# The order estimate of a mixed attention and recurrence kernel: the lo halves of the weights booked on VectorE instead of GpSimd

## The chip, the cores and the metric

The kernel runs on one core of a Trainium2 chip. The metric is the device time of one execution in microseconds (us), the median of several timed runs. A difference of 0.3% (about 2.6 us) is what a measurement of this kernel can tell from no change. The profile is one further execution, taken by the hardware profiler.

## The reference

One layer over 528 tokens (16 learned tokens ahead of 512) of width 1024. A projection with 5384 columns of the normalised input feeds three parts: an RWKV-7 recurrence (8 heads), a forgetting attention (8 heads) and two sigmoid gates. The two branches are projected, gated and added, go through another projection into the residual, and a squared-ReLU MLP of width 4096 follows.

```python
h = jnp.concatenate([meta_b, x], axis=1)
u = rmsnorm(h, norm_mix[l])
proj = u @ w_in[l]
gates = jax.nn.sigmoid((proj[..., C_RW + C_FX:] + b_gate[l]).astype(jnp.float32))
y_rw = rwkv7_branch(feat_rw, ...)      # S_t = S_{t-1} (diag(w_t) + a_t^T b_t) + v_t^T k_t
y_fx = fox_branch(feat_fx, ...)        # softmax(q k^T + F_q - F_k), causal
merged = gates[..., :D_MODEL] * (y_rw @ w_out_rw[l]) + gates[..., D_MODEL:] * (y_fx @ w_out_fx[l])
h = h + (merged @ w_o[l]).astype(h.dtype)
z = rmsnorm(h, norm_mlp[l])
h = h + (jnp.square(jax.nn.relu(z @ w_up[l])) @ w_down[l]).astype(h.dtype)
return h[:, N_META:]
```

## The kernel before

Every large product is made of three passes: an operand is split into a rounded part `hi` and a rest `lo`, and `hi*hi`, `hi*lo` and `lo*hi` are added in PSUM. For a weight tile of 128x512 ScalarE makes `whi` (a cast, L470) and VectorE `wlo` (raw minus `whi`, L471). A block of the input projection (128 output columns) takes 8 slices of the contraction, three matmuls each, over the tokens in one part (128x512) or two (128x264); these are the rows `pj` of L501.

Work in order of time: the norm and the first two blocks of the projection; then the **mixed stage** (from `turns.add` at L1017 to `turns.run()` at L1024), in which the other 40 blocks, the recurrence and the attention share the engines; then the gated output projections (`po` of L1060, L1092, L1109), and the MLP (L1139, L1257).

In the mixed stage TensorE's instructions stand in exactly the order in which the program issues them (`manual_schedule`, L1023). That order is chosen while the kernel is built, by `Turns.run` (L164). Each stream of work is a generator that yields a function telling when its next step could start. Ranks give precedence: 0 is the chain over the chunks, 1 the rest of the recurrence, 2 the attention, 3 its features, 4 the group norm, 8 the projections, which so fill what is left. `run` takes the first stream, by rank, whose estimated start (plus a small allowance per rank, `ROOM`) isn't later than TensorE's estimated time `ck.pe`; if there is none, it takes the earliest and moves `ck.pe` to it, so that the estimate has TensorE wait there.

The estimated times are kept by `Clock`. Its `read` (L98) goes over each new instruction, takes the time at which its inputs are ready, and books it on its engine: `RATE` (L67) has a fixed cost and a cost per column for VectorE (0.18 us + 1.06 ns), ScalarE (0.25 us + 0.85 ns) and GpSimd (0.30 us + 2.1 ns). `book` (L88) takes the first gap on the engine that is long enough; steps of rank 0 and 1 are `urgent` and may be booked ahead of something that is booked already. For a projection's step the estimate asks for the time of `whi` and `wlo` (`ck.ready(*w[k // 4])`, L495). The other engines' order, their semaphores and the DMA queues follow from the order of the program and a priority for the urgent steps.

The parts that the prediction speaks of:

- `pairs`: heads go in pairs through `keys` (`pkk` L735), `rows`, `scores` (`psr` L788, taken out of PSUM by VectorE at L789 and L791) and `keys_turned` (`pbt` L802). Two pairs make a group; there are two groups.
- `inverse` (L806), once for each group: it inverts triangular blocks. VectorE transposes (L821, after the last `pbt`, since its tile lies where `BK` lay), goes through 15 steps of two dependent instructions (L832, L833), transposes twice (L835, L836) and spreads the result into `Tt` and `Dn` (four instructions of L841). Only then TensorE's first `pw` (L847) can start.
- `attention`: scores `psc` L607, a softmax on VectorE and ScalarE (L616 to L623), transposes `ppt`/`ppm` (L636, L638), the product `py` (L649, L652).
- After the stage `yhi` and `ylo` (L1045) are made of the results, the gates `gl` are loaded (L1054) and go through a tanh (L1055), and the weights `wraw` of `wout` are loaded and split (L232 to L236). The tiles of this part lie in memory that the mixed stage used, so their first writers wait for its last readers: `ylo` for the last `pj` matmul that reads `uhi`, `gl` for the tiles of the attention.

Of the kernel before, what the change touches and what calls it, by code (L numbers as in the profile page):

```python
# [61 lines left out]
class Clock:  # L62
# [35 lines left out]
    def read(self):  # L98

        new = self.nc.cur_bb.bb.instructions[self.seen:]  # L100
        self.seen += len(new)
        for x in new:
            outs = [o.bass_ap for o in x.outs if hasattr(o, "bass_ap")]
            ins = [o.bass_ap for o in x.ins if hasattr(o, "bass_ap")]
            if not outs:
                continue
            for o in outs:
                t = o.tensor
                if hasattr(t, "cap_key") and t.name not in self.free:
                    ring, n = self.rings.setdefault(str(t.cap_key).rsplit("_", 2)[0], []), t.tag_meta.bufs  # L110
                    self.free[t.name] = self.last(ring[-n]) if len(ring) >= n else 0.0
                    ring.append(t.name)
            names = [a.tensor.name for a in ins]
            out = outs[0].tensor.name
            eng = "Pool" if out.startswith("wlo") else str(x.engine).split(".")[-1]

            def cols(a):
                return math.prod(n for _, n in a.ap[1:])
            deps = max([self.w.get(n, 0.0) for n in names] + [self.free.get(out, 0.0)])
            if eng == "PE":  # L120
                n = max(cols(outs[0]), 64)
                big = tuple(x.tile_size) == (128, 128)
                if ins[0].dtype == F32R:
                    cost = n / 2400 + 0.013
                else:
                    cost = n / 600 if big else n / 1200
                if self.form != tuple(x.tile_size):
                    self.form = tuple(x.tile_size)
                    cost += 0.1
                self.pe = end = max(self.pe, deps) + cost  # L130
            else:
                size = max([cols(a) for a in outs + (ins if "Reduce" in str(x.opcode) else [])])
                if eng in self.RATE and "DMA" not in str(x.opcode):
                    fixed, per = self.RATE[eng]
                    end = self.book(eng, max(deps, self.last(out)), fixed + per * size) + fixed + per * size
                else:
                    cost = 0.3 + size * 128 * 4 / 2.0e5
                    end = self.book("DMA", max(deps, self.last(out)), cost) + cost + 2.0
            for o in outs:
                self.w[o.tensor.name] = max(self.w.get(o.tensor.name, 0.0), end + self.HOP)  # L140
            for n in names:
                self.r[n] = max(self.r.get(n, 0.0), end + self.HOP)
# [1245 lines left out]
```

## Time and profile before

| | |
|---|---|
| time, median of 3 runs | 881.36 us (881.16 to 883.7) |
| the profiled execution: its time, its span | 884.7 us, 882.9 us |
| mean granted TensorE clock | 0.988 |
| busy in the span | TensorE 852.5, VectorE 619.7, ScalarE 459.1, GpSimd 122.1 us |
| mixed stage | about 36 to 448 us |
| output projections, MLP | about 450 to 548 us, 548 us to the end |

The profile's page gives busy time by engine, then 40 slices of the span, DMA queues, the chain of work that ended last, and groups of instructions with the idle time ahead of them and what ended it. The views of the trace used here: the list of who waited for whom; the timeline, whose rows have start and length in us, engine, line, operation, `out<-in`, shape, and in brackets the idle time before and what ended it; the chain of waits, whose pieces have start, length, engine and line; and busy time by stretch. Matmuls overlap, so a piece of several matmuls divided by their number is what one costs, not the duration that a single row shows. A `pj` matmul with fp32 operands split as above is one instruction; the small fp32 matmuls count twice or more in the trace (x24 in the trace for 12 in the program).

### The profile page before, as it was taken

The numbers are of one execution on the slowest core, as the hardware profiler recorded it, in microseconds if no ns is written. First come the engines' busy times: TensorE is split into PE (matmuls) and PEld (weight loads), VectorE is DVE, ScalarE is ACT, GpSimd is POOL, SyncE is SP. The second block draws the span as 40 slices with busy tenths as digits, with TensorE's granted clock in tenths as the row PEclk, the third lists the DMA queues.
The fourth block names the chain that finished last, engine by engine and source line by source line (L and its number), as shares of the span: only waits on it lengthen the run. The fifth ranks groups of instructions, "written<-read, shape, count | busy, mean of one in ns | idle before, by whom it ended". The sixth has DMA issues, their size and how long they took to land.

```text
span 882.9 us, 15881 instructions
## 1 busy us (share of the span) xinstructions
PE 852.5 (97%) x6040; PEld 695.1 (79%) x6040; DVE 619.7 (70%) x1222; ACT 459.1 (52%) x943; POOL 122.1 (14%) x129
## 2 busy tenths in 40 slices
PE   7899999999999999999979899999999999999998
PEld 6887887778887876778768688988888888887886
DVE  6985786657877846655566655677777778767787
ACT  7756443865564427654365553465445434534452
POOL 1111100101101000000002200200720270055000
PEclk9989999999999999999999999999999999999999
DMA  6131123121121322213077550562663274326331
GB/s 217 50 96 48 49 72 104 25 76 50 40 60 50 113 74 73 74 37 108 25 262 231 164 189 1 160 199 60 210 188 103 60 238 156 96 87 223 108 97 71
DMA packets 51340, 95.91 MB, mean 109 GB/s; under 512 B 5816, under 2 KB 6968, under 8 KB 51264
## 3 DMA queue, kind: packets, MB, share of 16 engines
q1 hardware_dynamic: 47680, 86.52, 31.1%
q0 software_dynamic: 1280, 4.20, 1.5%
q10 hardware_dynamic: 2304, 4.20, 1.3%
q8 instruction: 47, 0.77, 0.4%
q14 instruction: 29, 0.24, 0.1%
HBM read 88.57 MB, written 6.31 MB: 107 GB/s over the span
## 4 chain that ended last, share of the span: by engine, by line
PE 82%; DVE 6%; DMA 3%; ACT 2%; issue 1%; POOL 0%; SPq 0%; DVEq 0%; ACTq 0%; POOLq 0%
PE pj L501 27%; PE po L1139 20%; PE po L1257 11%; PE pd L1257 5%; PE po L1109 2%; PE po L1092 2%; PE pw L847 2%; PE psc L607 1%; DMA gl<-gd 1%; PE pbt L802 1%; PE py L652 1%; DMA wraw<-in_wup 1%; DVE L L791 1%; DMA wraw<-in_wout 1%; PE pssq L553 1%
## 5 line engine op out<-in xcount | busy, mean ns | idle before, releaser
L501 PE MATMUL pj<-uhi,whi 128*128 128x264 f32 (+1 forms) x480 | 167.9, 350 | 0.0
L501 PE MATMUL pj<-ulo,whi 128*128 128x264 f32 (+1 forms) x480 | 156.5, 326 | 2.6 <-DVE ulo L401 2.6
L501 PE MATMUL pj<-uhi,wlo 128*128 128x264 f32 (+1 forms) x480 | 156.1, 325 | 0.0
L501 PEld LDWEIGHTS pj<-uhi,whi 128*128 128x128 f32 x480 | 92.3, 192 | 19.8 <-issue 11.1
L501 PEld LDWEIGHTS pj<-ulo,whi 128*128 128x128 f32 x480 | 92.8, 193 | 7.1 <-DVE ulo L401 3.0
L501 PEld LDWEIGHTS pj<-uhi,wlo 128*128 128x128 f32 x480 | 92.5, 193 | 7.1
L236 DVE TENSOR_TENSOR wlo<-wraw,whi 128x512 fp32r<-128x512 f32 x88 | 71.3, 821 | 35.0 <-ACT whi L235 34.5
L1139 PE MATMUL po<-zhi,whi 128*128 128x512 f32 (+1 forms) x248 | 94.9, 383 | 0.6 <-ACT whi L235 0.6
L1139 PE MATMUL po<-zhi,wlo 128*128 128x512 f32 (+1 forms) x248 | 94.9, 383 | 0.0
L1139 PE MATMUL po<-zlo,whi 128*128 128x512 f32 (+1 forms) x248 | 94.8, 382 | 0.0
L471 DVE TENSOR_TENSOR wlo<-wraw,whi 128x512 fp32r<-128x512 f32 x80 | 56.6, 713 | 38.2 <-ACT whi L470 37.2
L235 ACT CAST whi<-wraw 128x512 fp32r<-128x512 f32 x88 | 53.9, 618 | 53.9 <-PE po L1139 21.3
L470 ACT CAST whi<-wraw 128x512 fp32r<-128x512 f32 x80 | 49.1, 619 | 37.1 <-PE pj L501 29.9
L270 ACT CAST whi<-t 128x512 fp32r<-128x512 f32 x64 | 40.0, 624 | 44.5 <-DVE wlo L271 20.6
L1257 PE MATMUL po<-wlo,fhi 128*128 128x512 f32 x160 | 62.8, 392 | 0.2 <-DVE wlo L271 0.2
L271 DVE TENSOR_TENSOR wlo<-t,whi 128x512 fp32r<-128x512 f32 x64 | 49.3, 784 | 18.9 <-ACT whi L270 18.0
L1257 PE MATMUL po<-whi,flo 128*128 128x512 f32 x160 | 62.4, 390 | 0.0
L1257 PE MATMUL po<-whi,fhi 128*128 128x512 f32 x160 | 61.9, 389 | 0.0
L1185 POOL TENSOR_TENSOR t<-traw 128x512 f32<-128x512 f32 x24 | 34.4, 1437 | 156.1 <-DVE wlo L271 137.4
L1139 PEld LDWEIGHTS po<-zhi,whi 128*128 128x128 f32 x248 | 46.6, 188 | 10.0 <-ACT whi L235 1.0
L1139 PEld LDWEIGHTS po<-zhi,wlo 128*128 128x128 f32 x248 | 46.6, 188 | 9.5 <-DVE wlo L236 0.4
L1139 PEld LDWEIGHTS po<-zlo,whi 128*128 128x128 f32 x248 | 46.6, 188 | 8.9
(299 smaller groups left out, 1779.4 us busy)
## 6 DMA issues: line engine op xcount, KB each, us to landing
wraw<-in_win SPq DMA_DIRECT2D x84, 256.0 KB, 2.6
wraw<-in_wup SPq DMA_DIRECT2D x64, 256.0 KB, 3.3
wraw<-in_wdn SPq DMA_DIRECT2D x48, 256.0 KB, 2.7
traw<-in_wdn SPq DMA_DIRECT2D x48, 256.0 KB, 3.3
gd<-gt ACTq DMA_DIRECT2D x16, 256.0 KB, 2.0
wraw<-in_wout SPq DMA_DIRECT2D x16, 256.0 KB, 4.3
gl<-gd SPq DMA_DIRECT2D x16, 256.0 KB, 3.3
wraw<-in_wo SPq DMA_DIRECT2D x16, 256.0 KB, 2.9
```

Of the source, the lines that this page charges most:

```text
L235: A.copy(hi, raw)
L236: low.tensor_tensor(lo, raw, hi.bitcast(F32), ALU.subtract)
L270: A.copy(hi, x)
L271: V.tensor_tensor(lo, x, hi.bitcast(F32), ALU.subtract)
L470: A.copy(hi, raw)
L471: low.tensor_tensor(lo, raw, hi.bitcast(F32), ALU.subtract)
L501: mm(po, a, b[:, k, a0:a1], start=n == 0, stop=n == 23)
L847: mm(ps_[hs, n - b0, :], lhs(n)[hs], rhs(n)[hs], start=True, stop=True)
L1092: mm(pd[i], a[:, k, 128 * i:128 * i + 128], b, start=k == 0 and n == 0, stop=k == 7 and n == 2)
L1139: mm(po[:, t0:t1], a, b[:, k, t0:t1], start=n == 0, stop=n == 23)
L1185: eng.tensor_tensor(t, sums[c, pair] if c in (T1, T2) else c, d, ALU.add)
L1257: mm(x[i], a[:, k, left, 128 * i:128 * i + 128], c, start=start and k == 0 and n == 0, stop=stop and k == n_pairs - 1 and n == 2)
```

## The change

One line of `Clock.read`. Before, an instruction that writes a tile whose name starts with `wlo` was booked on GpSimd, whatever engine executes it; now it is booked on the engine that executes it, VectorE. No instruction is added or removed. What changes is the estimate, and with it the order that `Turns.run` chooses.

```diff
@@ -112,7 +112,7 @@
             names = [a.tensor.name for a in ins]
             out = outs[0].tensor.name
-            eng = "Pool" if out.startswith("wlo") else str(x.engine).split(".")[-1]
+            eng = str(x.engine).split(".")[-1]
```

For a `wlo` of 512 columns the estimate was 0.30 + 512 x 2.1 ns = 1.38 us on a GpSimd with little booked; it is now 0.18 + 512 x 1.06 ns = 0.72 us on VectorE, among everything else that is booked there.

Three places of the new order. First, TensorE at the second group's inverse: what stands around the first `pw`, before:

```order
L501 MATMUL pj<-uhi,wlo 128x512
L847 MATMUL pw<-AX,Bm 64x64 x12
L501 MATMUL pj<-uhi,whi 128x512
L501 MATMUL pj<-ulo,whi 128x512
L501 MATMUL pj<-uhi,wlo 128x512
L649 MATMUL py<-pTm,vm 64x128 x2
```

and now:

```order
L501 MATMUL pj<-uhi,wlo 128x512
L847 MATMUL pw<-AX,Bm 64x64 x12
L553 MATMUL pssq<-fsq,cs 64x264 x4
L649 MATMUL py<-pTm,vm 64x128 x2
L652 MATMUL py<-pT,vt 64x128 x8
L501 MATMUL pj<-uhi,whi 128x264
```

Counted in the two orders, between the last `pbt` and this `pw` there stood 66 `pj` matmuls of 128x264 and 63 of 128x512, a `pbn`, a `pssq` and four `psc`; now there are 42 `pj` of 128x512, a `pbn` and two transposes of the attention (`ppm` and four `ppt` each), whose scores were moved ahead of the `psr`. At the first group's inverse there stood 72 of 128x264 and 48 of 128x512 (with `pbn`, `pssq`, `pv`); now 60 and 24 (with the same three). The second pair's `psr` of the second group, 36 in one piece before, are now 12 and 24 with 18 `pj` matmuls and a `pssq` between.

Second, VectorE in the middle of that inverse (`tmp` and `AX` are its tiles, `pe`, `nm`, `psc` and `rsum` the softmax of an attention block), before:

```order
L833 TENSOR_TENSOR AX<-AX,tmp 128x2x9x7
L618 ISA pe,nm<-psc,nF_3122 128x272
L618 ISA nm 128x1
L832 TENSOR_TENSOR tmp<-AX 128x128
L616 TENSOR_TENSOR psc<-psc,cs 128x128
L833 TENSOR_TENSOR AX<-AX,tmp 128x2x8x8
L618 ISA pe,nm<-psc,nF_3120,nm 128x256
L618 ISA nm 128x1
L832 TENSOR_TENSOR tmp<-AX 128x126
```

and now:

```order
L833 TENSOR_TENSOR AX<-AX,tmp 128x2x9x7
L832 TENSOR_TENSOR tmp<-AX 128x128
L833 TENSOR_TENSOR AX<-AX,tmp 128x2x8x8
L832 TENSOR_TENSOR tmp<-AX 128x126
L833 TENSOR_TENSOR AX<-AX,tmp 128x2x7x9
L832 TENSOR_TENSOR tmp<-AX 128x120
L471 TENSOR_TENSOR wlo<-wraw,whi 128x512
L833 TENSOR_TENSOR AX<-AX,tmp 128x2x6x10
```

The softmax has left the inverse; between L832 of the first step and L841 there are now three `wlo` and two copies `pT` (L640), where there were four `wlo`, the scaling of `qa` (L558) and the softmax. In the first group's inverse the same stands between the steps before and now: three `wlo` and the scaling of `ka`.

Third, ScalarE at the end of the mixed stage (`gt` takes the last gate block out of PSUM, `yhi` are the casts that the next products need). Before:

```order
L514 ACTIVATE gt<-pj,pr 128x512
L621 ACTIVATE pe,rsum<-pe,nm 128x528
L515 DMA gd_89<-gt 128x512
L653 COPY y_fx<-py 128x128
L641 COPY pTm<-ppm 16x128
L270 CAST yhi<-y_rw 128x512
L641 COPY pTm<-ppm 16x128
L270 CAST yhi<-y_rw 128x512 x3
L270 CAST yhi<-y_fx 128x512 x2
L653 COPY y_fx<-py 128x128
L270 CAST yhi<-y_fx 128x512 x2
L235 CAST whi<-wraw 128x512 x3
```

and now:

```order
L653 COPY y_fx<-py 128x128
L1055 ACT_TABLE_LOAD
L1055 ACTIVATE gl_5644<-gl_5644 128x512
L514 ACTIVATE gt<-pj,pr 128x512
L270 CAST yhi<-y_rw 128x512
L515 DMA gd_89<-gt 128x512
L270 CAST yhi<-y_rw 128x512 x3
L270 CAST yhi<-y_fx 128x512 x4
L235 CAST whi<-wraw 128x512 x2
```

The load of the tanh table, the first gate's tanh and the last `gt` now stand ahead of all eight casts. On TensorE the attention's last block (scores, two transposes, product) had three `pj` matmuls of 128x512 within it and ended the stage; now 33 stand within it and 18 more behind it. On SyncE's queue the first four loads of `gl` and that of the gain, which stood behind four loads of `wout` and two of `hres`, now stand ahead of them all. Counted over the whole order, the `pj` matmuls stood in 120 unbroken pieces and stand in 131. On TensorE nothing differs behind the first products of `wout`.

## Prediction

> **What bounds the kernel now.** I read the page first: the span, how busy each engine is, and in 40 slices the clock that TensorE was granted, in tenths.
>
> ```profile
> span 882.9 us, 15881 instructions
> PE 852.5 (97%) x6040; PEld 695.1 (79%) x6040; DVE 619.7 (70%) x1222; ACT 459.1 (52%) x943; POOL 122.1 (14%) x129
> PEclk9989999999999999999999999999999999999999
> ```
>
> TensorE is busy in 97% of the span. Since the change adds and removes no instruction, the time can move only by TensorE's waits, by its clock and by what an interrupted run of matmuls costs. The page doesn't tell where it waits, so I turned to the list of who waited for whom on TensorE (total, times, longest):
>
> ```profile
> PE psr L788 <- DVE L L791: 3.2, 4, 0.8
> PE po L1092 <- DVE gl L1062: 3.0, 2, 2.7
> PE psr L788 <- DVE Bm L789: 2.8, 4, 0.9
> PE po L1060 <- ACT whi L235: 2.5, 1, 2.5
> PE ppm L636 <- DVE pe L623: 1.9, 2, 1.2
> ```
>
> No row names `pw`: in the order of before, the two inverses are never waited for. In the whole mixed stage the waits come to little over 10 us of some 410, so that is all that any better order could gain there. Next I looked at what hides the inverses. The chain of waits (start, length, piece) between the last `pbt` and the first `pw` of each group is TensorE's own work from end to end:
>
> ```profile
> 87.58 9.71 PE pj L501 x78
> ...
> 107.07 1.49 PE pbt L802 x24
> ...
> 110.21 1.01 PE pbn L772 x4
> ...
> 115.06 1.04 PE pssq L553 x8
> ...
> 122.72 0.44 PE pv L577 x4
> 123.16 0.11 PE pvm L580
> 123.27 8.36 PE pj L501 x36
> 131.63 0.84 PE pw L847 x24
> ```
>
> ```profile
> 281.84 1.49 PE pbt L802 x24
> ...
> 309.49 0.84 PE pw L847 x24
> ```
>
> The first gap is 131.63 - 108.56 = 23.1 us, the second 309.49 - 283.33 = 26.2 us. The pieces also give prices: 9.71/78 = 0.1245 us for a `pj` of 264 columns, 8.36/36 = 0.232 us for one of 512. VectorE's timeline has the other side, from the transpose that the last `pbt` releases to the last of the four L841:
>
> ```profile
> 108.69 1.25 DVE L821 STREAM_TRANSPOSE AX<-Ain 128x1024 f32<-128x1024 f32 x1 [3.68 <-PE pbt L802]
> ...
> 127.37 1.41 DVE L841 TENSOR_SCALAR AX<-AX,even 128x576 f32<-128x576 f32 x2
> ```
>
> ```profile
> 283.46 1.25 DVE L821 STREAM_TRANSPOSE AX<-Ain 128x1024 f32<-128x1024 f32 x1 [2.11 <-PE pbt L802]
> ...
> 306.42 0.75 DVE L841 TENSOR_SCALAR AX<-AX,even 128x576 f32<-128x576 f32 x1
> ```
>
> The inverse is ready 128.78 - 108.56 = 20.2 us after the last `pbt` in the first group, 307.17 - 283.33 = 23.8 us in the second. So TensorE came 2.9 and 2.3 us late for it. Those two margins are what the new order has to live on.
>
> **The change, part by part.** *The inverses.* The new order leaves 60 `pj` of 264 and 24 of 512 columns, `pbn`, `pssq` and `pv` in the first gap: 60 x 0.1245 + 24 x 0.232 + 1.01 + 1.04 + 0.55 = 15.6 us. VectorE's queue there is the same as before (three `wlo` and one scaling between the steps), so the 20.2 us stand, and TensorE, whose matmuls are in a fixed order with `pw` next, waits 4.6 us (3.6 to 5.6). In the second gap are 42 `pj` of 512 columns, a `pbn` and two transposes of the attention, whose price is in the stage's last rows (start, us, engine, line):
>
> ```profile
> 443.67 0.28 PE L636 MATMUL ppm<-cs,pe 128*16 128x128 f32 x1 [0.73 <-DVE pe L623]
> 443.79 0.60 PE L638 MATMUL ppt<-cs,pe 128*128 128x128 f32 x4
> 445.57 0.28 PE L636 MATMUL ppm<-cs,pe 128*16 128x128 f32 x1 [1.19 <-DVE pe L623]
> ...
> 446.58 1.58 PE L652 MATMUL py<-pT,vt 128*64 128x128 f32 x16
> 450.64 0.68 PE L1060 MATMUL po<-yhi,whi 128*128 128x512 f32 x1 [2.48 <-ACT whi L235]
> ```
>
> 42 x 0.232 + 1.01 + 2 x 0.72 = 12.2 us. VectorE has lost the softmax here and keeps three `wlo` and two copies; that is the queue of the first inverse but for a copy, so I take its 20.2 us, and a wait of **8.0 us**. If the inverse took 23.8 us as before, it would be 11.6; without the roughly 2.5 us of foreign work in the queue, 5.5. What is queued behind the waiting `pw` is all of TensorE's work; nothing can go ahead of it. The matmuls that left the two gaps (7.5 and 14.0 us of work) aren't saved: they stand elsewhere in the stage, 48 more than before around and behind the last attention block.
>
> *The clock.* The stretches that the clock is granted in are 3.41 us long. Busy time by stretch (length, then PE busy, PEld, DVE, ACT, POOL, then PEclk):
>
> ```profile
> 61.67:65.08 3.41, 1.91 (x29) 1.35 (x30) 3.32 (x7) 0.00 (x0) 0.00 (x0) 1.00 0.38 145
> 65.08:68.50 3.42, 3.42 (x12) 2.60 (x10) 2.33 (x5) 2.14 (x3) 0.00 (x0) 0.50 0.00 0
> ...
> 225.50:228.90 3.40, 2.11 (x68) 1.66 (x62) 3.29 (x10) 0.00 (x0) 0.48 (x1) 1.00 0.38 130
> 228.90:232.30 3.40, 2.97 (x34) 2.48 (x27) 3.29 (x7) 1.58 (x2) 0.00 (x0) 1.00 0.02 5
> ```
>
> After a stretch with 1.91 us of TensorE busy the next one has half the clock; after one with 2.11 us it hasn't. A wait of 4.6 us, however it falls across two stretches, leaves one of them under 1.2 us busy. So each of the two waits is followed by at least one stretch at 0.50, which costs 3.41/2 = 1.7 us of matmuls: +3.4 us (1.7 to 5.1). The Trainium skill's page "TensorE: Matmul & The Clock Gate" (section "What's actually happening") has the clock halved only after an idle window of about 3.4 us; by that the first wait would seldom do it. The trace differs, with 1.91 us busy in a stretch that was followed by 0.50.
>
> *The end of the stage.* Before, TensorE's last `py` ends at 446.58 + 1.58 = 448.16 and the first `po` starts 2.48 us later, once ScalarE has done its casts. ScalarE and SyncE there:
>
> ```profile
> 442.80 0.67 ACT L514 ACTIVATE gt<-pj,pr 128x512 f32<-128x512 f32 x1
> ...
> 446.17 1.66 ACT L270 CAST yhi<-y_rw 128x512 fp32r<-128x512 f32 x3
> ...
> ...
> 453.67 1.28 ACT L1055 ACT_TABLE_LOAD   x1 [2.04 <-DMA gl<-gd]
> 454.96 1.15 ACT L1055 ACTIVATE gl<-gl 128x512 f32<-128x512 f32 x2
> ```
>
> ```profile
> 450.29 1.78 SPq L1054 DMA_DIRECT2D gl<-gd  x4
> ```
>
> Now `py` ends 18 `pj`, or 4.2 us, before TensorE's last matmul; call that last end E. The first `gl` load is issued at E - 4.2 and lands 453.67 - 450.29 = 3.4 us later; then come the table load (1.28) and a tanh (0.58), to E + 1.1; `gt` (0.67); eight casts of 0.55 (1.66/3), to E + 6.2; a `whi` of the same length, to E + 6.8. That is 4.3 us more than 2.48, and with a `wlo` that the third matmul now needs, **+4.5 us**. If the gate's load is there by E, it is +3.2; and the 2.7 us for which the last of these products waited (L1092) may go, since the gates are loaded earlier: down to +0.5. Up to +6.5 if the weights, queued behind five loads now, land late.
>
> *What is won.* The first two waits of the last rows above, 0.73 and 1.19 us, have 18 and more `pj` over them. The second group's second `psr` is split by 18 `pj` and a `pssq`, over 3 us, and one chain step gets work before its `pch`:
>
> ```profile
> 275.73 0.44 PE L788 MATMUL psr<-L,BK 64*64 64x128 f32 x4 [0.95 <-DVE Bm L789]
> 276.98 0.87 PE L788 MATMUL psr<-L,BK 64*64 64x128 f32 x20 [0.81 <-DVE L L791]
> ```
>
> ```profile
> 211.39 0.45 PE L907 MATMUL pch<-uv,L 128*64 128x64 f32 x8 [0.64 <-DVE uv L930]
> ```
>
> Together 0.73 + 1.19 + 0.95 + 0.81 + 0.64 = **-4.3 us** (-3 to -5). The other three `psr` still stand in one piece and wait as before.
>
> *More interruptions.* 131 pieces of `pj` instead of 120. Three `pj` of 512 columns between other work take
>
> ```profile
> 390.13 0.89 PE pj L501 x3
> ```
>
> instead of 3 x 0.232 = 0.70, so 0.19 for each interruption, **+2.1 us** (0 to 3).
>
> The sum: 4.6 + 8.0 + 3.4 + 4.5 - 4.3 + 2.1 = +18.3 us. The profiled execution took 884.7 us, 1.8 us outside its span, so it would be 903.0; it lies 3.3 us over the median of the timed runs, which I carry over: 881.4 + 18.3 = **899.7 us**.
>
> **The rivals.** *VectorE is in time.* If the inverse were ready 12.2 us after the last `pbt` in the second group and 15.6 in the first, both waits and the halved clock would go: 18.3 - 12.6 - 3.4 = +2.3 us, 883.7, no slower than a measurement can tell. The queue with the softmax gone speaks for it; against it, the two dependent instructions of 15 steps, three transposes and four spreads alone filled most of 20.2 us where no softmax stood between. It decides from about 8 us less than that.
>
> *The second inverse stays at 23.8 us*, because what sets it is the dependence between its steps and not the softmax: 3.6 us more, 903.3. Against it: the first group did the same steps in 20.2.
>
> *The clock falls only after a stretch that is idle throughout*, as the page on the clock gate has it. The 8.0 us hold a whole stretch, the 4.6 us do only if it starts in their first 1.2 us: one stretch at half clock less, -1.7, 898.0. The rows at 61.67 and 225.50 speak against it.
>
> That the change does nothing is excluded: the order of TensorE differs throughout the stage.
>
> **How the numbers follow.** Forecast (899.7) 0.67; second inverse at 23.8 us (903.3) 0.13; clock only after full idleness (898.0) 0.10; VectorE in time (883.7) 0.10. With the bounds, the low ends 3.6 + 5.5 + 1.7 + 0.5 - 5 + 0 give +6.3, or 887.7, and the high ends 5.6 + 11.6 + 5.1 + 6.5 - 3 + 3 give +28.8, which all at once is unlikely: the range is 887.5 to 908. The rival in time is left out of it, and about as much beyond the upper end. A measurement of this kernel tells about 0.3% from no change, 2.6 us. VectorE in time is mostly "same", a third of it faster; so faster 0.03, same 0.06, slower 0.91.
>
> **What would show it.** In the changed kernel's waits a row `pw` L847 waiting for L841 of VectorE, twice, with 4 to 5 and about 8 us; after each a stretch with clock 0.50, so a mean clock below 0.988; no `ppm` waiting at the stage's end; the first `po` of L1060 6 to 7 us after the last `pj`, with ScalarE's table load ahead of `gt`. If `pw` waits are missing or under 3 us in sum, the forecast is wrong at its main term. If they are there and the time is under 890 us, what is wrong is the end of the stage or the price of the fill.

## The result and the profile after

The changed kernel takes 903.87 us (median of 4 runs, 902.3 to 904.64) where the kernel before took 881.74 beside it (4 runs): a ratio of 1.0242, 95% interval 1.0222 to 1.0263. By the two medians that is 22.1 us more, by the ratio 21.3. The profiled execution took 904.22 us against 884.7 before, 19.5 us more, at a mean clock of 0.974 instead of 0.988. The difference between 22.1 and 19.5 is that the profiled execution of before lay 3.0 us over the median, that of after 0.4 us.

The page of the changed kernel, the same rows as before:

```profile
span 902.4 us, 15888 instructions
PE 859.7 (95%) x6040; PEld 700.0 (78%) x6040; DVE 618.6 (69%) x1222; ACT 458.6 (51%) x943; POOL 123.0 (14%) x129
PEclk9999989898999889999999999999999999999999
```

TensorE's share has fallen from 97% to 95%, and the clock's row has five 8s where it had one. Who waited for whom on TensorE (total, times, longest):

```profile
PE pw L847 <- DVE AX L841: 12.3, 2, 8.1
PE po L1060 <- ACT whi L235: 5.7, 1, 5.7
...
PE psr L788 <- DVE L L791: 2.4, 3, 0.8
PE ppt L636 <- ACT sg L255: 2.2, 1, 2.2
...
PE po L1109 <- DVE hres L1100: 1.8, 1, 1.8
PE pch L928 <- DVE uv L915: 1.5, 1, 1.5
...
PE psr L788 <- DVE Bm L789: 1.1, 2, 0.9
...
PE po L1092 <- DVE gl L1062: 0.7, 2, 0.4
```

The reader is to see three things. `pw`, absent before, leads the list with 12.3 us. `po` of L1060 has gone from 2.5 to 5.7. And other rows have shrunk: `psr` from 6.0 to 3.5 in its two rows, `po` of L1092 from 3.0 to 0.7, `ppm` from 1.9 to nothing. All rows of the list add up to 38.8 us, those of before to 26.3: 12.5 of the 19.5 us are waits. The other 7.0 are time in which TensorE's matmuls ran slower or stood further apart.

The second inverse on VectorE, and then both waits on TensorE, of the changed kernel (start, length, engine, line; the idle time ahead in brackets):

```profile
293.42 1.25 DVE L821 STREAM_TRANSPOSE AX<-Ain 128x1024 f32<-128x1024 f32 x1 [1.45 <-PE pbt L802]
...
300.64 0.69 DVE L471 TENSOR_TENSOR wlo<-wraw,whi 128x512 fp32r<-128x512 f32 x1
...
303.71 0.68 DVE L471 TENSOR_TENSOR wlo<-wraw,whi 128x512 fp32r<-128x512 f32 x1
...
306.26 0.68 DVE L471 TENSOR_TENSOR wlo<-wraw,whi 128x512 fp32r<-128x512 f32 x1
...
312.17 1.33 DVE L841 TENSOR_SCALAR AX<-AX,even 128x576 f32<-128x576 f32 x2
```

```profile
123.58 1.54 PE L847 MATMUL pw<-AX,Bm 64*64 64x64 f32 x24 [4.19 <-DVE AX L841]
...
305.13 0.39 PE L501 MATMUL pj<-uhi,wlo 128*128 128x512 f32 x1
313.64 1.55 PE L847 MATMUL pw<-AX,Bm 64*64 64x64 f32 x24 [8.12 <-DVE AX L841]
```

The last `pbt` of the two groups end at 103.3 and 293.3, as the chain of waits has it, and `pw` starts 20.3 us later both times, as soon as the inverse is ready. The waits are 4.19 and 8.12 us. In the middle of the second inverse VectorE finds room for three `wlo` between the dependent steps. TensorE's fill is spent at 305.5 us all the same, since its order has nothing else ahead of `pw`.

Busy time by stretch around the second wait (length, PE, PEld, DVE, ACT, POOL busy, then PEclk):

```profile
302.60:306.00 3.40, 2.92 (x13) 2.05 (x11) 3.12 (x11) 1.24 (x3) 0.00 (x0) 1.00 0.41 102
306.00:309.40 3.40, 0.00 (x0) 0.00 (x0) 3.23 (x9) 0.54 (x1) 0.00 (x0) 1.00 0.40 148
309.40:312.80 3.40, 0.00 (x0) 0.00 (x0) 3.40 (x6) 0.30 (x1) 0.00 (x0) 0.50 0.43 158
312.80:316.20 3.40, 2.56 (x30) 2.14 (x32) 1.54 (x4) 0.39 (x2) 0.00 (x0) 0.50 0.05 16
316.20:319.60 3.40, 3.40 (x25) 2.06 (x22) 0.77 (x1) 1.59 (x4) 0.00 (x0) 0.50 0.00 0
319.60:323.10 3.50, 3.50 (x26) 3.26 (x28) 0.00 (x0) 0.18 (x1) 0.00 (x0) 0.50 0.02 5
323.10:326.50 3.40, 3.40 (x56) 3.13 (x53) 0.92 (x2) 0.38 (x1) 0.00 (x0) 1.00 0.00 0
```

The clock is halved for four stretches, 13.65 us, not for one. The first of them is idle and costs nothing; the row of `pw`, 0.91 us long in the timeline of before, became 1.55, and the matmuls behind it ran at half speed to 323.1. Even the stretch from 316.2, in which TensorE is busy throughout, is followed by another at 0.50.

### The profile page after: what moved, and what is told of

It is laid out like the page before. It is cut to its first block, busy times and chain, and to the rows that moved or that the text cites. A ratio compares the mean times of both kernels' runs of the same rounds, so it can differ in the third digit from the quotient of the medians.

```text
span 902.4 us, 15888 instructions
## 1 busy us (share of the span) xinstructions
PE 859.7 (95%) x6040; PEld 700.0 (78%) x6040; DVE 618.6 (69%) x1222; ACT 458.6 (51%) x943; POOL 123.0 (14%) x129
## 4 chain that ended last, share of the span: by engine, by line
PE 78%; DVE 9%; DMA 3%; ACT 3%; issue 2%; POOL 1%; ACTq 0%; DVEq 0%; POOLq 0%; SPq 0%
PE pj L501 24%; PE po L1139 19%; PE po L1257 11%; PE pd L1257 5%; PE po L1109 2%; PE pw L847 2%; PE psc L607 1%; DMA gl<-gd 1%; PE py L652 1%; DMA wraw<-in_wo 1%; PE pbt L802 1%; PE ppt L638 1%; PE pssq L553 1%; DVE L L791 1%; DMA wraw<-in_wup 1%
## 5 line engine op out<-in xcount | busy, mean ns | idle before, releaser
L501 PE MATMUL pj<-uhi,whi 128*128 128x264 f32 (+1 forms) x480 | 170.2, 355 | 0.0
L236 DVE TENSOR_TENSOR wlo<-wraw,whi 128x512 fp32r<-128x512 f32 x88 | 68.8, 794 | 33.0 <-ACT whi L235 32.7
L471 DVE TENSOR_TENSOR wlo<-wraw,whi 128x512 fp32r<-128x512 f32 x80 | 55.9, 701 | 36.7 <-ACT whi L470 31.6
L270 ACT CAST whi<-t 128x512 fp32r<-128x512 f32 x64 | 39.9, 624 | 44.5 <-DVE wlo L271 20.6
```

What stands on the lines that cost most here:

```text
L236: low.tensor_tensor(lo, raw, hi.bitcast(F32), ALU.subtract)
L270: A.copy(hi, x)
L471: low.tensor_tensor(lo, raw, hi.bitcast(F32), ALU.subtract)
L501: mm(po, a, b[:, k, a0:a1], start=n == 0, stop=n == 23)
```

## The experiments

**Theory.** The new order leaves too little fill ahead of the two `pw`. TensorE waits there, and the clock that falls in the waits slows what comes behind by more than the 3.4 us of the prediction. **Rivals:** the lost time lies in the new order elsewhere; or the clock costs one halved stretch for each wait, as predicted.

### Which half of the change empties the gaps

The change does two things to the estimate: `wlo` occupies VectorE's lane, and its ready time is worked out there. Each can be done alone. In `load_only` the lane is occupied, but the ready time still comes from GpSimd's:

```diff
                 if eng in self.RATE and "DMA" not in str(x.opcode):
                     fixed, per = self.RATE[eng]
+                    if out.startswith("wlo"):
+                        self.book(eng, max(deps, self.last(out)), fixed + per * size)
+                        eng, (fixed, per) = "Pool", self.RATE["Pool"]
```

> Half of the change: wlo occupies VectorE's lane in the estimate as in the changed kernel, but the time at which it counts as ready still comes from GpSimd's lane, as before. Counted in the order, 23.2 and 23.1 us of fill then stand in the two gaps ahead of the first pw (before 22.6 and 25.8, changed 15.5 and 12.2). Theory (what shrank the fill is the ready time: the estimate takes wlo to be late while the inverse holds VectorE's lane, finds no projection that could start, and lets TensorE idle to the pw): no pw wait over 1 us, time within 4 us of before, 878 to 885. Rival (the load on the lane is what matters, by moving everything else of VectorE): pw waits again, over 895.

In `ready_only` the ready time is VectorE's, and the lane stays free:

```diff
+    def book(self, eng, at, cost, keep=True):
...
+        if keep:
+            bisect.insort(sp, (at, at + cost))
...
+                    end = self.book(eng, max(deps, self.last(out)), fixed + per * size, not out.startswith("wlo")) + fixed + per * size
```

> The other half: the ready time of wlo is worked out on VectorE's lane, but wlo doesn't occupy it. Fill in the gaps by the order: 11.4 and 14.5 us. With an inverse of 20.3 us: pw waits of 8.9 and 5.8 us. Theory: 14.7 us of waits and 5 to 10 us of halved clock, 900 to 906. Rival (the ready time alone does no harm): under 890.

`load_only` took 879.78 us, ratio to before 0.9964 (0.9932 to 0.9996): no loss at all. `ready_only` took 911.24, ratio 1.0323 (1.0269 to 1.0377), more than expected. Its first waits:

```profile
PE pw L848 <- DVE AX L842: 12.0, 2, 7.0
...
PE pyt L968 <- DVE y_rw L961: 5.5, 1, 5.5
```

The `pw` waits came to 7.0 and 5.0 us where 8.9 and 5.8 were worked out, and in the middle of the stage, at 214.1 us, the group norm's transposes `pyt` end a wait of 5.5 us that wasn't foreseen. In `load_only` no row names `pw`. So the ready time alone does the harm, and the rival of `load_only`, the occupied lane, falls.

Why, the estimate itself shows when its numbers are written out while each kernel is built. In the changed kernel it has TensorE idle for 6.2 and 9.9 us ahead of the two `pw`, in `ready_only` for 9.3 and 7.9; before and in `load_only` for none. The steps of the inverse are urgent and follow each other by 0.15 us in the estimate, so a `wlo` of 0.72 us finds no gap on VectorE's lane until the inverse is over. No projection may start before that: the next one could at 102.1 and 299.6 us of the estimate's time, the two `pw` at 100.6 and 297.4, which are therefore the earliest steps left. On the chip VectorE took three `wlo` in between, as the rows above show. The estimate gave up the fill for operands that were there.

### What the waits cost beside their length

`busy_wait`: TensorE works through the waits. `fill_first` and `fill_second` do it at one of them.

```diff
                 ps_ = psm(name)[:, :384]
+                if fill:
+                    ck.read()
+                    for _ in range(fill):
+                        mm(ps_, uhi[:, 0, :128], uhi[:, 1, :384], start=True, stop=True)
+                    ck.seen = len(nc.cur_bb.bb.instructions)
...
+                p1 = six("pw", b0, ..., (0 if b0 else 44 if g else 22))
```

> The changed kernel's order, but TensorE is given throwaway matmuls of 384 columns ahead of the first pw of each inverse (22 and 44, some 3.9 and 7.8 us by the price of a pj matmul), so that it is busy for about as long as it waited (4.2 and 8.1 us). The pw waits should shrink to under 0.8 us each while the work after them starts no earlier. Theory (the halved clock after the two waits is the mis-sized term; in the changed kernel's trace the half-clock stretches at 121.7 and 309.4 us lengthen their matmuls by 3.3 and 7.0 us): the clock stays at 1.00 there and the time falls by about 10 us, to 893.6. Rival (each wait costs one halved stretch, 1.7 us, and the other lost clock belongs to the new order elsewhere): about 3.4 us less, 900.5.

> Throwaway matmuls (22 of 384 columns) ahead of the first pw of the first inverse only; the second still waits 8.1 us. With both filled the time fell by 1.0242 - 1.0134 = 1.1%, 9.5 us, 7.2 us of it between the first pw and the second group's last pbt and 4.3 between the second pw and the last pj by the traces. Theory (each wait has its own clock price): 9.5 x 7.2/11.5 = 6.0 us less than the changed kernel, 898; from the second pw to the last pj still about 152. Rival (the 7.2 us was the position of the stretches in one execution, not the first wait): 1.7 to 3.4 us less, 900 to 902.

> The other half: 44 throwaway matmuls ahead of the first pw of the second inverse only; the first still waits 4.2 us. Theory: 9.5 x 4.3/11.5 = 3.5 us less than the changed kernel, 900; the stretches after 309 us at full clock, and 148 us from the second pw to the last pj instead of 152. Rival (the 8.1 us wait is the dear one, 13.65 us at half clock after it): 7 us less, 897.

`busy_wait` took 895.93 us, ratio 1.0134 (1.0091 to 1.0178). Against the changed kernel's 1.0242 that is 1.08% of 882, 9.5 us less (give or take 4, by the two intervals), with work in place of the waits. Its waits and its stretches behind the second `pw`:

```profile
PE pw L853 <- DVE AX L841: 1.5, 2, 0.8
```

```profile
306.80:310.20 3.40, 3.40 (x55) 2.55 (x56) 1.30 (x3) 1.85 (x5) 0.00 (x0) 1.00 0.02 5
310.20:313.60 3.40, 3.40 (x46) 3.19 (x45) 0.88 (x2) 0.03 (x1) 0.00 (x0) 1.00 0.00 0
```

Of the 12.3 us of waiting 1.5 are left, and both stretches behind the `pw` are at 1.00, where the changed kernel's were at 0.50. The theory's 10 us is met; not all of it belongs to the two waits, as shown below. And the price doesn't divide as expected: `fill_first` took 900.33, ratio 1.0198 (1.0156 to 1.0240), 3.9 us less than the changed kernel, a time within its rival's 900 to 902; `fill_second` 903.59, ratio 1.0235 (1.0198 to 1.0272), 0.6 us less, although its clock is whole behind the wait:

```profile
314.20:317.60 3.40, 2.60 (x42) 1.67 (x42) 1.79 (x4) 1.21 (x3) 0.00 (x0) 1.00 0.08 24
```

So the rival that made the second wait the dear one falls: its 897 lies below the interval, which starts at 899.5. In `fill_second`'s trace the stretch from the second `pw` to the last `pj` is 148.3 us instead of 152.6, as the theory has it, but 1.6 us are lost ahead of that `pw`, 1.4 at the first `po` and 1.0 behind it. 3.9 + 0.6 is less than 9.5, though within what the intervals allow.

`before_late` makes the same waits in the order of before:

```diff
             V.transpose(At, X.rearrange("p t j -> p j t"))
+            ck.read()
+            for _ in range(5 if g else 3):
+                V.transpose(At, X.rearrange("p t j -> p j t"))
+            ck.seen = len(nc.cur_bb.bb.instructions)
```

> The order of before on TensorE, with the last transpose of the inverse repeated (3 times in the first group, 5 in the second) without the estimate knowing of it: about 7 and 10.5 us more on VectorE, against margins of 2.9 and 2.3 us, so pw waits of about 4 and 8 us as in the changed kernel, and nothing else of the change. Theory: waits 12 plus some 10 us of halved clock, 881.5 + 22 = about 903. Rival (one halved stretch for each wait): 881.5 + 12 + 3.4 = 897.

900.83 us, ratio 1.0194 (1.0145 to 1.0242), 17.1 us more than before: between the theory's 22 and the rival's 15.4. The interval (12.8 to 21.3 us) holds the rival's figure and just leaves out the theory's.

```profile
PE pw L851 <- DVE AX L845: 7.3, 2, 4.3
...
PE pj L501 <- DVE wlo L471: 4.9, 1, 4.9
```

The waits are 12.2 us as intended, though 4.9 of them fell on a `pj` in the second gap, whose `wlo` the repeated transposes had pushed back. 17.1 - 12.2 leaves 4.9 us for the clock, give or take 4. Of the same kind of wait two measurements thus give 4.9 and 9.5 us; only the second is clear of the prediction's 3.4.

`after_again` is the changed kernel, unedited:

> The changed kernel once more, to see whether its halved stretches are tied to the program. The waits should be the same within 0.2 us (4.2 and 8.1 us for pw). Theory (the clock is decided on a grid of 3.41 us that doesn't start with the program, and a wait of 2 to 5 us halves a stretch only if it falls well within one): the halved stretches after the shorter waits (at 156, 210, 234 us) come and go, that after the 8.1 us wait stays, time 902 to 906. Rival (they belong to the order): the same stretches again.

903.59 us, ratio 1.0237 (1.0184 to 1.0289), the same `pw` waits of 12.3 us. Two stretches of each execution, first of after, then of `after_again`:

```profile
207.00:210.40 3.40, 1.93 (x34) 1.39 (x34) 3.32 (x8) 2.07 (x6) 0.00 (x0) 1.00 0.49 142
210.40:213.80 3.40, 3.00 (x29) 2.37 (x29) 2.56 (x8) 2.71 (x8) 1.66 (x3) 0.51 0.05 17
```

```profile
207.00:210.40 3.40, 2.32 (x24) 1.85 (x22) 3.32 (x6) 3.25 (x9) 0.00 (x0) 1.00 0.26 76
210.40:213.80 3.40, 2.38 (x41) 1.98 (x41) 3.17 (x10) 2.15 (x7) 1.12 (x2) 1.00 0.30 83
```

The same work falls otherwise on the grid of stretches, and the 6.83 us at half clock that after has from 210.4 don't occur; the ones after the `pw` waits and after the `ppt` wait of 2.2 us (from 156) do. The theory of a grid that doesn't start with the program holds. The stretch from 234 is replaced by a longer one from 231.7, two come that after hasn't (from 64.5 and 289.8), and behind the second wait three stretches were halved instead of four.

The traces settle what the medians leave open. Behind the two waits of the changed kernel the stretches at half clock are, added up:

```profile
121.70:128.50 6.80, 4.92 (x34) 4.04 (x35) 5.06 (x17) 1.31 (x5) 0.00 (x0) 0.50 0.33 99
309.40:323.10 13.70, 9.46 (x78) 7.46 (x80) 5.71 (x9) 2.47 (x6) 0.00 (x0) 0.50 0.13 44
```

Half of the time in which TensorE was busy there is what the halved clock can have cost: (4.92 + 9.46)/2 = 7.2 us. The 10 us of the expectation counted idle time as well. In `after_again` the same working gives 4.4 us (3.40 and 5.48 us busy), in `before_late` 4.6 (5.46 and 3.80). For all halved stretches of an execution it gives 9.9 us before, 18.8 after, 17.9 in `after_again` and 5.8 in `busy_wait`, which also lacks the stretches from 210.4 and 234.3 us of after, 5.0 us by the same working. Take the listed waits, this price and the throwaway matmuls off the span, and 845 to 847 us are left in each of the fourteen traces: waits and halved clock account for the whole difference, and the changed order (844.9 for 846.7 before) costs nothing beyond them.

### Taking the waits away

`short_inverse` keeps TensorE's order and shortens what it waits for:

```diff
                 m, w = 15 - s, s + 1
+                if s:
+                    ck.read()
+                    ck.phantom(tmp.tensor.name, [AX_.tensor.name], 2 * m * w)
+                    ck.phantom(AX_.tensor.name, [AX_.tensor.name, tmp.tensor.name], 2 * m * w)
+                    continue
```

> TensorE's order of the changed kernel, with 14 of the 15 steps of each inverse left out on VectorE, so that the inverse is some 8 us shorter (what it computes is then not the inverse); the estimate still counts them. The first pw wait (4.2 us) should be gone and the second (8.1 us) be at most about 0.5 us. Theory (waits 12.3 plus 10.3 us of halved clock after them): 903.9 - 22 = about 882. Rival (clock 3.4 us, the rest lost elsewhere in the new order): 903.9 - 12.3 - 3.4 = 888.

`phantom` books the step in the estimate as if it were there. 887.06 us, ratio 1.0038 (1.0009 to 1.0066). No row of `pw` is left:

```profile
PE po L1073 <- ACT whi L243: 5.7, 1, 5.7
```

18.0 us of the 21.3 are gone (1.0242 - 1.0038 of 882), 5.7 beyond the 12.3 of waiting. The rival's figure (888) is nearer than the theory's (882). What is left over before shows in the trace: its listed waits add up to 1.0 us more than those of before, and its halved stretches cost 3.0 us more by the working above.

`pw_late` keeps the changed rates and has the estimate put more ahead of `pw`:

```diff
-                yield lambda: max(ck.ready(Dn), banks(1))
+                yield lambda f=9.0 if b0 == 0 else 0.0: max(ck.ready(Dn) + f, banks(1))
```

> The changed kernel with 9 us added, in the estimate alone, to the time at which the first pw of each inverse could start, so that other work is put ahead of it: 24.0 and 21.1 us of fill by the order. Theory (the two pw waits and the clock after them are the loss): both waits under 1 us, time 903.9 - 12.3 - 10 = 881.6. Rival (the new order costs elsewhere): over 888.

883.97 us, ratio 1.0009 (0.9979 to 1.0040), no `pw` row: the loss is gone within the measurement, as the theory has it (20.6 us less than the changed kernel). Its order is no longer the changed kernel's, so it shows that the loss can be avoided with the changed rates; that the changed order costs little elsewhere rests on `short_inverse` and on the sums of the traces.

### The end of the stage

`casts_first` moves one thing on ScalarE:

```diff
+                th = act(g, g, AF.Tanh, scale=0.5)
+                if m == 0:
+                    after(th, cast)
```

> The changed kernel with one thing moved on ScalarE: the load of the tanh table and the first tanh stand behind the eight casts yhi instead of ahead of them. Theory (the 5.7 us wait of the first po is made of the chain table load, tanh, gt, eight casts, whi after the last pj): the wait falls by the 1.3 us of the table load and the 0.5 us of the tanh, to about 3.9 us, and the time to 902.1. Rival (the casts are released by the last pj itself, whose tiles they overwrite, and wait anyway): 903.9, no change.

905.36 us, ratio 1.0242 (1.0201 to 1.0284): no change, the time of the rival. ScalarE in the changed kernel, then in `casts_first`:

```profile
465.11 1.28 ACT L1055 ACT_TABLE_LOAD   x1 [2.58 <-DMA gl<-gd]
466.41 0.63 ACT L1055 ACTIVATE gl<-gl 128x512 f32<-128x512 f32 x1
466.94 0.67 ACT L514 ACTIVATE gt<-pj,pr 128x512 f32<-128x512 f32 x1
467.51 0.61 ACT L270 CAST yhi<-y_rw 128x512 fp32r<-128x512 f32 x1
...
471.66 1.14 ACT L235 CAST whi<-wraw 128x512 fp32r<-128x512 f32 x2
```

```profile
466.79 0.69 ACT L514 ACTIVATE gt<-pj,pr 128x512 f32<-128x512 f32 x1 [4.12 <-PE pj L501]
467.38 0.61 ACT L1045 CAST yhi<-y_rw 128x512 fp32r<-128x512 f32 x1
...
472.73 1.28 ACT L1056 ACT_TABLE_LOAD   x1
```

The gate's load had landed at 465.1, 1.5 us ahead of the last `pj`'s end at 466.6, so the table load and most of the tanh lie beside TensorE's last matmuls. Behind `gt`, which that end releases, stand the eight casts and a `whi`; from the start of `gt` at 466.9 to the first `po` at 472.3 these make 5.4 of the 5.7 us. The wait fell by the other 0.3 us in `casts_first`, and the table load moved behind a `whi`. Since `gt` stands ahead of the casts in both orders, whether the casts themselves would have waited for the last `pj`, as the rival has it, is not shown.

### A version that beats both

`load_only` fills the gaps but leaves no `pj` for the stage's end, where its attention waits:

```profile
PE ppt L639 <- DVE pe L626: 3.5, 2, 3.1
...
PE ppm L639 <- DVE pe L626: 1.2, 1, 1.2
```

A larger booked cost keeps more for the end:

```diff
-                        self.book(eng, max(deps, self.last(out)), fixed + per * size)
+                        self.book(eng, max(deps, self.last(out)), 1.25 * (fixed + per * size))
```

> The half of the change that only occupies VectorE's lane, with each wlo booked there at 1.25 times its estimated cost. By the order, 23.8 and 25.7 us of fill stand in the two gaps, and 60 pj matmuls (0 with the factor 1, 3 in before, 51 in the changed kernel) stand within and behind the attention's last block. Theory (a fill kept for the stage's end takes its waits, 4.7 us with the factor 1, and the clock halved there for 13.65 us): no pw wait over 1 us, no ppt or ppm wait over 1 us at the stage's end, no stretch at half clock there before the last pj, time 879.8 - 8 = about 872, faster than before. Rival (what is kept for the end is missing earlier, and the waits and halved stretches come there): 878 to 884.

> The same with the factor 1.3: fill 23.8 and 24.0 us in the gaps, 21 pj matmuls behind the last scores. Theory: between the kernel with the factor 1 (879.8) and the one with 1.25, about 875. Rival: 878 to 884, as the next one.

`load_125` took 876.05 us (before beside it 883.33), ratio 0.9918 (0.9897 to 0.9939); `load_130` 878.06, ratio 0.9930 (0.9906 to 0.9955). Both beat the kernel before, by 7.2 and 6.2 us, by less than expected; 878.06 is the edge of the rival's range. The longest of the later waits of `load_125`, whose span is 873.9 us:

```profile
PE po L1063 <- ACT yhi L273: 4.6, 1, 4.6
```

No `pw`, `ppt` or `ppm` row is left. All rows add up to 21.7 us, 4.6 less than before; its halved stretches cost 6.9 us by the working above, 3.1 less than before. That is 7.7 of the 9.0 us by which its span is shorter. Against `load_only`, whose rows add up to 21.8, the waits gained nothing: the first `po`, now 4.6 us (0.4 in `load_only`, 2.5 before), takes back what `ppt` and `ppm` gave. What differs between these two traces is the clock, 6.9 us for 13.8, and how much of that is the fill at the stage's end and how much the position of the stretches isn't shown. Two halved pairs remain, one from 241.0 us and one behind the last `pj`.

## Why the prediction was right

The direction, the place and the mechanism were right, and 903.87 lies in the range; the predicted 899.7 was 4.2 us low. For the profiled execution the sum was 18.3 and the measured difference 19.5 us. That they are so close is partly luck: the stage's end was taken too high and the interruptions too, the clock too low, and waits came that the sum didn't have. By its steps:

- **The `pw` waits: right.** 4.2 and 8.1 us for 4.6 and 8.0. The step that carried most, that the second inverse without the softmax takes what the first did, held: 20.3 us from the last `pbt` to `pw` both times. With it the rivals of an inverse in time and of one at 23.8 us fall.
- **The halved clock: right as a mechanism, sized too small.** The sum had one stretch at 0.50 behind each wait, +3.4 us (1.7 to 5.1). In the trace of after two and four stretches were halved, the first of the four idle, which comes to 7.2 us; in `after_again` to 4.4. The trace of after has 7.0 us beside the listed waits for the clock and the interruptions together, where the sum had 3.4 + 2.1, and all its halved stretches cost 8.9 us more than those of before. The first stretches were counted, but not that the clock stays down behind them, nor that stretches behind shorter waits (the `ppt` of 2.2 us, the `pch` of 1.5) are halved in some executions too.
- **The clock only after full idleness: wrong.** The stretch ahead of the first halving was not idle throughout:

```profile
118.30:121.70 3.40, 1.09 (x5) 0.56 (x3) 3.40 (x4) 1.51 (x3) 0.00 (x0) 1.00 0.34 109
121.70:125.10 3.40, 1.51 (x26) 1.43 (x26) 2.34 (x5) 0.30 (x1) 0.00 (x0) 0.50 0.55 166
```

  With 1.09 us busy in it, the next is at 0.50. The Trainium skill's page "TensorE: Matmul & The Clock Gate" (section "What's actually happening") also has work that starts on a throttled clock back at the full one after its first 3.4 us or so. Here it took longer: from `pw` at 313.64 us TensorE was busy without a break for 9.46 us before the clock was whole, the row from 316.20 among them, 3.40 us busy and followed by 0.50. The same section of the Trainium skill calls the window free-running, not reset when a kernel starts. What `after_again` shows agrees: the halving at the first `pw` wait starts there at 125.9 us, in after at 121.7.
- **The end of the stage: sized at +4.5, measured +3.2** (5.7 for 2.5). The term that failed is the late gate load: it was issued at 462.4 us, 4.2 ahead of the last matmul's end as worked out, but landed 2.7 us later instead of 3.4, early enough for the table load to be over by that end. The prediction's own alternative, "If the gate's load is there by E, it is +3.2", is what happened. The wait of L1092 went as it might (3.0 to 0.7); a wait for `hres` (1.8) took most of its place.
- **What is won: the named waits went** (`ppm` 1.9, `psr` 2.5 less; of the `pch` of 0.6 us 0.4 stayed), about the -4.3 of the sum. Two came that it didn't have: `ppt` 2.2 and `pch` 1.5.
- **Interruptions, +2.1: no sign of them.** They weren't measured alone. But the span of after less its waits and its halved clock is 844.9 us, that of before 846.7, so there is no room for a cost of 2.1 that isn't won back elsewhere. `short_inverse`, with the new order and no `pw` wait, gives 846.9.

The last 2.9 us of the miss come from carrying the profiled execution over to the median: that of before lay 3.3 us over the 881.4 that the prediction had, that of after 0.4 over its own.

## What to carry to other kernels

An estimate that orders work may become worse when one of its numbers becomes truer: here the right engine made `wlo` late in the model, because the model can't put it between the steps of an urgent chain, as the engine does. When such a table changes, count the fill that stands between the start of a long side computation and the first instruction that needs it, and set it against the computation's length in the trace; the two differences, 4.6 and 8.0 us, were the larger part of the result before anything ran. To the waits of TensorE add what the clock takes behind them, which here came to about four to six tenths of them (4.4 and 7.2 us for 12.3 in two executions of one kernel, 4.6 for 12.2 in another).

## What the runs showed of the hardware

The clock is decided on stretches of 3.41 us whose grid doesn't start with the program: in two executions of the same kernel the halved stretches began at 121.7 and at 125.9 us for the same first wait, and a pair from 210.4 us occurred in one only. From within an 8.1 us wait on the clock stayed halved for 13.65 us in one execution and 10.24 in the other, with TensorE busy 2.56, 3.40 and 3.50 us of the last three stretches in the first. In `load_only` it stayed halved for four stretches in which TensorE was busy throughout, after one with 2.21 us busy:

```profile
96.70:100.10 3.40, 2.21 (x45) 1.48 (x38) 3.31 (x7) 0.00 (x0) 0.00 (x0) 1.00 0.25 90
100.10:113.80 13.70, 13.70 (x71) 11.38 (x71) 5.70 (x10) 4.17 (x12) 1.11 (x2) 0.50 0.08 23
```

In the changed kernel a stretch with 2.24 us busy was followed by a halved one, where the trace of before has one with 2.11 that was not; busy time alone doesn't decide it:

```profile
152.40:155.80 3.40, 2.24 (x80) 1.78 (x78) 1.28 (x3) 3.07 (x7) 0.14 (x1) 1.00 0.28 96
155.80:159.20 3.40, 2.33 (x9) 1.84 (x9) 0.56 (x1) 2.85 (x8) 0.00 (x0) 0.50 0.47 140
```
